# Order of the attention heads in the second half of a two-branch decoder layer, with its side products spread anew and one scaling moved to ScalarE

## The chip, the cores and the metric

One core of a Trainium2 chip runs the whole layer in one launch. The metric is the device time of that execution in microseconds. PE is TensorE (matmuls), PEld its weight loads, DVE VectorE, ACT ScalarE, POOL GpSimd, SP SyncE, which here issues the DMAs.

## The reference

The input x is 2048 tokens of 1024 channels in fp32. After an RMS norm, one projection gives queries, keys, values and gates of two attention branches and two more gates of 1024 columns each:

```python
h = rms_norm(x, pre_norm_g)
(sb_q, sb_k, sb_v, sb_z, df_q, df_k, df_v, df_z, g_sb, g_df) = split_cols(h @ w_in)
# stick-breaking branch, 8 heads of 64, block of queries against all keys before them
z = q @ k.T * scale
a = exp(log_sigmoid(z) - suffix)        # suffix: sum of softplus(z) over the later keys
y_sb = ((a @ v) * silu(sb_z)) @ w_o_sb
# differential branch, 4 heads, two score maps each, ALiBi bias, causal
p = softmax(s + bias)
y_df = (rms_norm((p[0] - lam * p[1]) @ v, subln_g) * 0.8 * silu(df_z)) @ w_o_diff
merged = sigmoid(g_sb + b) * y_sb + sigmoid(g_df + b) * y_df
out = x + rms_norm(merged @ w_out, post_norm_g)
```

## The kernel before, in words

Products are made in a split form: an operand is kept as a rounded part and a rest, and a product is the sum of three (or two) matmuls. A projection of 128 columns for 512 tokens is 24 matmuls (8 chunks of channels by 3), and one call of a generator makes one of them; a pair of calls covers the 1024 tokens of a half and shares one loaded weight tile (`load_w`, tags `w_hi` and `w_lo`, two buffers each).

The sequence is worked in two halves of 1024 tokens. In each, the list `heads` (line 1056) names the attention heads in order: a stick-breaking entry is a pair of heads (names s00 to s13, the first digit being the half), a differential one is a head with two maps (d00 to d13). While one is in attention, the projections of the next are interleaved (q, k, v and, for stick-breaking, z), in the order of the letters of `ORDER`. The letter S in it stands for the side steps: the differential gates' projections (z, 8 calls a half) and those of the two merge gates (g, 32 calls a half). `SIDES` says how many of the 40 fall to each of the eight entries of a half. In the second half the last 16 steps (`LAST_G`) are ordered by token group: eight for the first 512 tokens, then eight for the others, each with its own weight load.

Stick-breaking attention (`sb_group`): scores into PSUM, a sigmoid on ScalarE, a running product on VectorE (`a_R`, a scan), split into two f16 parts (`a_W`), a transposing DMA (`a_P`), a scaling copy to fp32r (`a_h`; three of four by ScalarE, the fourth by GpSimd), the product with the values (`a_O`). Differential attention (`df_row`): scores, bias and maximum on VectorE, exponentials on ScalarE (`f_row`), then row 1 scaled by `l2` and added to row 0. Chunks of even number do that in one VectorE instruction, chunks of odd number in two on GpSimd. `df_pair` transposes the sum on TensorE (`f_T`), splits it (`f_h`, `f_l`) and multiplies (`f_O`).

Behind the last head stands the merge of 256 tokens at a time (`merge`: products `y` with w_o, gates by a sigmoid; `finish`: products `o` with w_out and the norm). Its first four groups of tokens need only the first half's results. The matrix w_o is loaded in two halves into the buffers of the normed input (`load_wo`): the first when the last head starts, the second when the last side step is recorded. w_out (`load_wout`) goes to the buffers of the attention. In the last head the side steps are spread over the first 70% of its work.

The program is recorded first (`Recorder`), then put in order (`plan`): a list scheduler that knows a cost for every instruction (`cost`), and, for each buffer tag, how many of the next tiles in line may be taken (`FREE`: three for the PSUM tag "pj" of projections and of `y`, one otherwise). `issue` writes the instructions out in that order, and each engine runs its own in order.

Of the kernel before, what the change touches and what calls it, by code (L numbers as in the profile page):

```python
# [13 lines left out]
AF = mybir.ActivationFunctionType  # L14
ALU = mybir.AluOpType
# [19 lines left out]
FBANKS = ("S", "T", "S", "T", "S", "O", "pj")  # L35
HBANKS = (("S", "T"), ("S", "T"))
XTAGS = (("V",) * 4, ("row", "row", "row", "pre"))
SIDES = ((4, 4, 4, 4, 4, 4, 4, 12), (4, 4, 4, 4, 4, 4, 4, 12))
LAST_G = (2, 8)
SCALE = 0.125  # L40
LAMBDA_INIT = 0.2
SLOPES = [2.0 ** (-8.0 * (h + 1) / NDIFF) for h in range(NDIFF)]
BIG = 1e30
RSCALE = 2.0 ** 15
OFF = dict(sb_q=0, sb_k=512, sb_v=1024, sb_z=1536, df_q=2048, df_k=2560, df_v=3072, df_z=3584, g=4096)


# [84 lines left out]
class Recorder:  # L132


    def __init__(self, nc):
        self.nc, self.ops, self.lane, self.fifo, self.hold = nc, [], 0, {}, None
        for e in ENGINES:
            setattr(self, e, _Engine(self, e))

    def tile(self, pool, shape, dtype, name, tag=None, bufs=None, depth=None):  # L140
        t = Tile_(pool, tag, bufs, shape, dtype, name)
        if depth:
            t.free = self.fifo.setdefault((id(pool), tag), [depth, [], depth])
        return View(t)
# [65 lines left out]
def cost(o):  # L210

    v = o.outs[0] if o.outs else o.ins[0]
    n = 1
    for k in (o.ins[0] if o.call in ("tensor_reduce",) else v).shape[1:]:
        n *= k
    if o.engine == "tensor":
        t = 109.0 if o.call == "transpose" else 5 + 0.4415 * max(n, 256)
        return t, n / 2.4 + 215
    psum = any(x.tile.tag in ("S", "T", "O", "pj") for x in o.ins)
    if o.engine == "scalar":  # L220
        t = 80 + 0.833 * n + (80 if any(isinstance(o.kw.get(k), View) for k in ("scale", "bias")) else 0)
        if "accum_out" in o.kw:
            return t + 130, t + 260
        return t, t + 100
    if o.engine == "vector":
        if n <= 8:
            return 195.0, 200.0
        if o.call == "tensor_tensor_scan":
            t = 60 + 2.36 * n
        elif o.call in ("tensor_scalar", "tensor_scalar_mul", "tensor_scalar_add", "tensor_copy", "memset") and not psum:  # L230
            t = 130 + 0.7 * n
        elif o.call == "tensor_tensor_reduce":
            return 75 + 1.06 * n, 230 + 1.06 * n
        else:
            t = (75 if psum else 135) + 1.07 * n
        return t, t + 75
    if o.engine == "gpsimd":
        if any(isinstance(a, View) for a in o.args[2:]) and o.call == "tensor_scalar":
            return 280 + 2.5 * n, 330 + 2.5 * n
        t = {"tensor_tensor": 100 + 2.3 * n, "tensor_sub": 100 + 2.3 * n, "tensor_add": 100 + 2.3 * n, "memset": 180 + 0.2 * n}.get(o.call, 190 + 0.9 * n)  # L240
        return t, t + 50
    if o.kw.get("transpose"):
        return 1250.0, 3400.0
    size = 4.0 * 128 * n
    return 70.0, 2100 + size / 150

FREE = {"pj": 3}
# [6 lines left out]
def plan(rec):  # L256

    import heapq

    now, order = 0.0, []  # L260
    free = dict.fromkeys(ENGINES, 0.0)
    waiting = {e: [] for e in ENGINES}
    ripe = {e: [] for e in ENGINES}
    events, n_event = [], 0
    dma = 0.0
    live = {}
    blocked = {}
    port = {"vector": 0.0, "gpsimd": 0.0}

    def can_take(o):  # L270
        for t in o.new:
            q = t.free
            if q is None or t.real == "held":
                continue
            if q[0] <= 0 or t not in q[1][:FREE.get(t.tag, 1)]:
                return q
        return None

    def offer(o):
        heapq.heappush(waiting[o.engine], (o.ready + o.spare, o.n, o))  # L280
        heapq.heappush(events, o.ready)
        heapq.heappush(events, o.ready + o.spare)

    for o in rec.ops:
        if not o.left:
            offer(o)
    done = 0
    while done < len(rec.ops):
        progress = False
        for e in ENGINES:  # L290
            if free[e] > now:
                continue
            w, r = waiting[e], ripe[e]
            while w and w[0][0] <= now:
                _, _, o = heapq.heappop(w)
                heapq.heappush(r, (o.prio, o.n, o))
            put_back, took = [], None
            while r:
                x = heapq.heappop(r)
                q = can_take(x[2])  # L300
                if q is None:
                    took = x[2]
                    break
                blocked.setdefault(id(q), (q, []))[1].append(x)
            if took is None:
                early = min((x for x in w if x[2].ready <= now and can_take(x[2]) is None), default=None)
                if early is None:
                    continue
                w.remove(early)
                heapq.heapify(w)  # L310
                took = early[2]
            o = took
            progress = True
            o.start = max(now, port["gpsimd" if e == "vector" else "vector"]) if o.port else now
            free[e] = o.start + o.took * MARGIN[e]
            if o.port:
                port[e] = free[e]
            if e == "sync":
                dma = max(dma, now) + (o.lag - 2100) * 0.6
                o.end = dma + 2100  # L320
            else:
                o.end = o.start + o.lag * MARGIN[e]
            order.append(o)
            done += 1
            for t in o.new:
                if t.free is not None:
                    t.free[1].remove(t)
                    t.free[0] -= 1
                    wake(blocked, t.free, ripe, heapq)
            for s in (*o.succ.values(), *o.behind.values()):  # L330
                spare = 0.0
                if s.n in o.behind:
                    at = now
                elif s.engine == e and e != "sync":
                    at = free[e]
                else:
                    at, spare = o.end + HOP, SAFE[s.engine]
                    if s.engine == "tensor" and s.call == "transpose":
                        at += STATIONARY
                s.spare = max(s.ready + s.spare, at + spare)  # L340
                s.ready = max(s.ready, at)
                s.spare -= s.ready
                s.left -= 1
                if not s.left:
                    offer(s)
            for t in {v.tile for v in (*o.outs, *o.ins)}:
                t.users -= 1
                live[t] = max(live.get(t, 0.0), o.end)
                if not t.users and t.free is not None:
                    n_event += 1  # L350
                    heapq.heappush(events, live[t] + HOP)
                    heapq.heappush(blocked.setdefault("ends", []), (live[t] + HOP, n_event, t.free))
            heapq.heappush(events, free[e])
        if progress:
            continue
        assert events, stuck(blocked)
        now = max(now, heapq.heappop(events))
        ends = blocked.get("ends", [])
        while ends and ends[0][0] <= now:
            q = heapq.heappop(ends)[2]  # L360
            q[0] += 1
            wake(blocked, q, ripe, heapq)
    return order
# [27 lines left out]
def hybrid_layer(ctx: ExitStack, tc: tile.TileContext, x, pre_g, w_in, b_gate, lq1, lk1, lq2, lk2, subln_g, w_o_sb, w_o_df, w_out, post_g, out):  # L391
# [329 lines left out]
    def sb_group(p, hf, hd, gl, K, V, q, u):  # L721
# [4 lines left out]
        for kc in range(G, -1, -1):  # L726
            edge = kc == G
            ends = sm([P, 4], F32, name=f"{n}_e{kc}", tag="ends")
            for half in range(2):
# [25 lines left out]
                for j in range(nj):  # L755
# [2 lines left out]
                    hl = T([P, 2, CQ], F32R, f"{n}_h{kc}{half}{j}", tag)  # L758
                    if c0:
                        nc.gpsimd.memset(hl[:, :, :c0].bitcast(F32), 0.0)  # L760
                    if j == 3:
                        nc.gpsimd.tensor_scalar(hl[:, :, c0:], post[:, j, :, c0:], 1.0 / RSCALE, 0.0, ALU.mult, ALU.add)
                    else:
                        nc.scalar.activation(hl[:, :, c0:], post[:, j, :, c0:], AF.Copy, scale=1.0 / RSCALE)
                    lhs = V[kc // 2][:, (kc % 2) * 4 + j, :]
# [11 lines left out]
    def sb_attend(p, hf, st):  # L777
        us = [T([P, CH], F32, f"u{hf}{p}{gl}", "u") for gl in range(2)]
        zs = zb_dram[p][:, hf * HALF:(hf + 1) * HALF]
        early = (hf, p) not in ((0, 3), (1, 1))  # L780
        if early:
            zt = T([P, 2, CH], F32, f"uz{hf}{p}", "bm")
            nc.sync.dma_start(zt, zs)
# [41 lines left out]
    def df_row(d, hf, ii, st, bias, l1):  # L825
# [37 lines left out]
        for k, (c, w) in enumerate(ck):  # L863
# [1 line left out]
            if k % 2 == 0:  # L865
                nc.vector.scalar_tensor_tensor(a, b, l2, a, ALU.mult, ALU.add)
            else:
                nc.gpsimd.tensor_scalar(b, b, l2, None, ALU.mult)
                nc.gpsimd.tensor_add(a, a, b)
        return {(c + o) // P: rows[0][k][:, o:o + P] for k, (c, w) in enumerate(ck) for o in range(0, w, P)}  # L870

# [176 lines left out]
    with tc.tile_pool(name="wpool", bufs=2, reuse_waits="tile") as wpool, tc.tile_pool(name="att", bufs=1, reuse_waits="tile") as apool:  # L1048
# [4 lines left out]
        build_h(0, 0, xs[0])  # L1053
        load_constants()
        xs.append(load_x(0, 1, XTAGS[1]))
        heads = [(hf, sb, i) for hf, sb, pairs in ((0, 1, range(4)), (0, 0, range(4)), (1, 1, range(2)), (1, 0, range(4)), (1, 1, range(2, 4))) for i in pairs]
        project = lambda hf, sb, i: (sb_project if sb else df_project)(i, hf)

        def do(f):
# [14 lines left out]
        for k, (hf, sb, i) in enumerate(heads):  # L1074
# [46 lines left out]
                sides = side(1)  # L1121
            st = st2
        assert not sides
        M = merge(0, wo)
        rec.hold = None
        wt = load_wout()
# [37 lines left out]
```

## Time and profile before

| | |
|---|---|
| median of 3 runs | 2184.78 us (2184.68 to 2186.52) |
| the profiled execution | 2185.57 us |
| its span, first to last instruction | 2183.8 us |
| TensorE busy in the span | 2077.5 us, 95% |
| VectorE, ScalarE, GpSimd busy | 62%, 56%, 40% |
| mean granted TensorE clock | 0.982 |

The span is what the trace shows; the time holds 1.8 us more around it. Matmuls are pipelined and a record's end is modelled, so a busy TensorE is not yet one at its peak; the number of instructions in a stretch says more.

### The profile page before, as it was taken

The numbers are of one execution on the slowest core, as the hardware profiler recorded it, in microseconds if no ns is written. First come the engines' busy times: TensorE is split into PE (matmuls) and PEld (weight loads), VectorE is DVE, ScalarE is ACT, GpSimd is POOL, SyncE is SP. The second block draws the span as 40 slices with busy tenths as digits, with TensorE's granted clock in tenths as the row PEclk, the third lists the DMA queues.
The fourth block names the chain that finished last, engine by engine and source line by source line (L and its number), as shares of the span: only waits on it lengthen the run. The fifth ranks groups of instructions, "written<-read, shape, count | busy, mean of one in ns | idle before, by whom it ended". The sixth has DMA issues, their size and how long they took to land.

```text
span 2183.8 us, 34416 instructions
## 1 busy us (share of the span) xinstructions
PE 2077.5 (95%) x11136; PEld 1766.1 (81%) x11136; DVE 1356.7 (62%) x3142; ACT 1220.9 (56%) x2937; POOL 876.9 (40%) x1086
## 2 busy tenths in 40 slices
PE   5999999999999999999989999999998978999998
PEld 5888888888888888777878888888876767988997
DVE  6546655656557467777776767776775575434344
ACT  4556565644444478888655555656886674322221
POOL 2556566655354124444434243433444564111110
PEclk9999999999999999999999999999999989999999
DMA  5987988854564479979523232325899987444542
GB/s 157 273 235 207 272 210 247 225 189 163 190 237 162 135 190 206 200 167 203 150 63 118 70 112 78 104 72 151 194 231 247 285 165 184 141 144 134 161 131 87
DMA packets 474083, 376.26 MB, mean 172 GB/s; under 512 B 309552, under 2 KB 391472, under 8 KB 473904
## 3 DMA queue, kind: packets, MB, share of 16 engines
q1 hardware_dynamic: 473904, 374.07, 62.7%
q8 instruction: 88, 1.44, 0.3%
q14 instruction: 91, 0.75, 0.1%
HBM read 168.44 MB, written 117.44 MB: 131 GB/s over the span
## 4 chain that ended last, share of the span: by engine, by line
PE 42%; ACT 6%; DMA 5%; DVE 3%; issue 2%; POOL 1%; SPq 1%; DVEq 0%; ACTq 0%; POOLq 0%
PE y L384 7%; PE o L384 7%; PE g L384 6%; DMA a_P<-a_W 4%; PE f_S L384 3%; PE f_O L384 3%; PE a_O L384 2%; PE a_S L384 2%; PE f_T L384 2%; ACT f_row L384 1%; ACT a_h L384 1%; SPq L384 1%; ACT a_W L384 1%; DMA u<-ul_dram 1%; DVE f_row L384 1%
## 5 line engine op out<-in xcount | busy, mean ns | idle before, releaser
L384 POOL TENSOR_TENSOR a_W<-a_R,a_W 128x512 f16<-128x512 f32 (+1 forms) x160 | 182.7, 1143 | 225.4 <-ACT a_W L384 205.9
L384 ACT ACTIVATE a_h<-a_P 128x512 fp32r<-128x512 f16 (+1 forms) x448 | 244.0, 606 | 33.8 <-DMA a_P<-a_W 20.4
L384 DVE TENSOR_TENSOR_SCAN a_R<-a_S,a_e,high 128x512 f32<-128x512 f32 x192 | 237.7, 1269 | 35.5 <-ACT a_S L384 20.6
L384 ACT ACTIVATE f_row<-f_row,f_mx 128x512 f32<-128x512 f32 (+3 forms) x320 | 206.9, 652 | 51.0 <-DVE f_mx L384 50.8
L384 PE MATMUL y<-u,woh 128*128 128x256 f32 x1024 | 209.8, 284 | 3.4 <-DVE y04g L384 2.3
L384 PE MATMUL g<-hh,g_w_hi 128*128 128x512 f32 x512 | 203.5, 397 | 3.7 <-ACT g_s L384 2.2
L384 PE MATMUL g<-hh,g_w_lo 128*128 128x512 f32 x512 | 203.9, 398 | 1.3 <-DMA g_w_lo<-g_w_d 1.2
L384 PE MATMUL o<-wt,m 128*128 128x512 f32 x672 | 203.9, 396 | 0.0
L384 PE MATMUL g<-hl,g_w_hi 128*128 128x512 f32 x512 | 203.4, 397 | 0.0
L384 ACT ACTIVATE a_W<-a_R 128x512 f16<-128x512 f32 (+2 forms) x320 | 174.2, 556 | 28.3 <-DMA a_P<-a_W 22.1
L384 DVE CUSTOM_DVE_ANT_0 f_row<-f_S,f_bm 128x512 f32<-128x512 f32 (+3 forms) x304 | 167.1, 573 | 34.1 <-PE f_T L384 16.6
L384 PEld LDWEIGHTS y<-u,woh 128*128 128x128 f32 x1024 | 169.7, 191 | 11.3 <-issue 3.0
L384 DVE TENSOR_TENSOR a_W<-a_R,a_W 128x512 f16<-128x512 f32 (+2 forms) x160 | 115.8, 725 | 100.6 <-ACT a_W L384 98.7
L384 POOL TENSOR_SCALAR f_row<-f_row,f_l 128x512 f32<-128x512 f32 (+2 forms) x64 | 109.5, 1711 | 153.3 <-DVE f_l L384 149.1
L384 ACT ACTIVATE f_h<-f_T 128x512 fp32r<-128x512 f32 (+2 forms) x176 | 81.9, 497 | 128.1 <-PE f_T L384 55.0
L384 PE MATMUL y<-u,wol 128*128 128x256 f32 x512 | 142.5, 283 | 0.0
L384 PEld LDWEIGHTS o<-wt,m 128*128 128x128 f32 x672 | 123.1, 190 | 23.4
L384 DVE TENSOR_TENSOR f_l<-f_T,f_h 128x512 fp32r<-128x512 f32 (+2 forms) x176 | 94.8, 565 | 68.5 <-ACT f_h L384 66.6
L384 DVE TENSOR_TENSOR_SCAN a_R<-a_R,high 128x128 f32<-128x128 f32 (+3 forms) x128 | 112.8, 910 | 35.7 <-POOL a_R L384 34.9
L384 ACT ACTIVATE a_S<-a_S 128x512 f32<-128x512 f32 x192 | 107.9, 578 | 34.2 <-PE a_S L384 32.9
L384 POOL TENSOR_SCALAR a_h<-a_P 128x512 fp32r<-128x512 f16 (+1 forms) x128 | 83.4, 652 | 82.8 <-PE a_O L384 37.9
L384 PEld LDWEIGHTS g<-hh,g_w_hi 128*128 128x128 f32 x512 | 97.1, 190 | 21.6 <-ACT g_s L384 3.5
(1182 smaller groups left out, 5622.2 us busy)
## 6 DMA issues: line engine op xcount, KB each, us to landing
g_dram<-g_s SPq DMA_DIRECT2D x64, 256.0 KB, 3.1
g_w_hi<-g_w_d SPq DMA_DIRECT2D x24, 512.0 KB, 3.7
g_w_lo<-g_w_d SPq DMA_DIRECT2D x24, 512.0 KB, 5.0
g_w_raw<-in_w_in_dram SPq DMA_DIRECT2D x32, 256.0 KB, 4.0
g_w_d<-g_w_hi SPq DMA_DIRECT2D x16, 512.0 KB, 4.1
g_w_d<-g_w_lo SPq DMA_DIRECT2D x16, 512.0 KB, 4.4
u<-uh_dram SPq DMA_DIRECT2D x64, 128.0 KB, 3.2
u<-ul_dram SPq DMA_DIRECT2D x64, 128.0 KB, 3.4
```

The costliest lines, as they stand in the source:

```text
L384: i = getattr(getattr(rec.nc, o.engine), o.call)(*map(real, o.args), **{k: real(v) for k, v in o.kw.items()}).ins
```

## The change

In the second half the four stick-breaking entries come first and the four differential ones behind them; before, two stick-breaking ones stood on either side of the differential ones. The side steps of that half are 5, 5, 5, 5, 4, 4, 4, 8 instead of seven times 4 and 12. The stick-breaking entry that stands ahead of a differential one is now s13, so s13 loads its gate late (`early`) and s11 early. The odd chunks of row 1 are scaled by ScalarE; the addition stays on GpSimd. In the planner, a DMA issue costs 420 ns instead of 70, a transposing one 1320 instead of 1250, and tiles carry a stage: a tile of the merge can't be taken while an earlier stage's tile of the same tag is still in line. `SHARE` writes the old choice of engine for the copy of the fourth block as a table and changes nothing.

```diff
-SIDES = ((4, 4, 4, 4, 4, 4, 4, 12), (4, 4, 4, 4, 4, 4, 4, 12))
+SIDES = ((4, 4, 4, 4, 4, 4, 4, 12), (5, 5, 5, 5, 4, 4, 4, 8))
+SHARE = ((0, 0, 0, 1), (0, 0, 0, 1))
...
-        self.nc, self.ops, self.lane, self.fifo, self.hold = nc, [], 0, {}, None
+        self.nc, self.ops, self.lane, self.fifo, self.hold, self.stage = nc, [], 0, {}, None, 0
...
         t = Tile_(pool, tag, bufs, shape, dtype, name)
+        t.stage = self.stage
...
     if o.kw.get("transpose"):
-        return 1250.0, 3400.0
+        return 1320.0, 3400.0
     size = 4.0 * 128 * n
-    return 70.0, 2100 + size / 150
+    return 420.0, 2100 + size / 150
...
-            if q[0] <= 0 or t not in q[1][:FREE.get(t.tag, 1)]:
+            if q[0] <= 0 or t not in q[1][:FREE.get(t.tag, 1)] or q[1][0].stage != t.stage:
                 return q
...
-                    if j == 3:
-                        nc.gpsimd.tensor_scalar(hl[:, :, c0:], post[:, j, :, c0:], 1.0 / RSCALE, 0.0, ALU.mult, ALU.add)
+                    if SHARE[half][j]:
+                        (None, nc.gpsimd, nc.vector)[SHARE[half][j]].tensor_scalar(hl[:, :, c0:], post[:, j, :, c0:], 1.0 / RSCALE, 0.0, ALU.mult, ALU.add)
...
-        early = (hf, p) not in ((0, 3), (1, 1))
+        early = (hf, p) not in ((0, 3), (1, 3))
...
-                nc.gpsimd.tensor_scalar(b, b, l2, None, ALU.mult)
+                nc.scalar.activation(b, b, AF.Copy, scale=l2)
                 nc.gpsimd.tensor_add(a, a, b)
...
-        heads = [(hf, sb, i) for hf, sb, pairs in ((0, 1, range(4)), (0, 0, range(4)), (1, 1, range(2)), (1, 0, range(4)), (1, 1, range(2, 4))) for i in pairs]
+        heads = [(hf, sb, i) for hf, sb, pairs in ((0, 1, range(4)), (0, 0, range(4)), (1, 1, range(4)), (1, 0, range(4))) for i in pairs]
...
         assert not sides
+        rec.stage = 1
         M = merge(0, wo)
```

## Rows read from the trace of the kernel before

**Rows 1.** The page: TensorE's share, then granted clock and DMA in 40 slices.

```profile
PE 2077.5 (95%) x11136; PEld 1766.1 (81%) x11136; DVE 1356.7 (62%) x3142; ACT 1220.9 (56%) x2937; POOL 876.9 (40%) x1086
...
PEclk9999999999999999999999999999999989999999
DMA  5987988854564479979523232325899987444542
```

**Rows 2.** Busy time by head: s10, s11, d10 to d13, s12, s13 in two parts.

```profile
core 0: us, PE busy (x) PEld busy (x) DVE busy (x) ACT busy (x) POOL busy (x), PEclk, DMA share, GB/s
765.40:907.00 141.60, 140.68 (x714) 118.12 (x713) 96.05 (x126) 112.03 (x257) 51.47 (x71) 1.00 0.85 198
907.00:1039.50 132.50, 119.84 (x582) 97.62 (x581) 97.63 (x113) 111.54 (x257) 58.88 (x78) 0.94 0.86 186
1039.50:1139.90 100.40, 94.22 (x511) 79.58 (x511) 74.39 (x230) 60.50 (x154) 37.38 (x40) 0.98 0.40 110
1139.90:1264.10 124.20, 120.26 (x674) 102.45 (x673) 90.62 (x282) 68.85 (x187) 49.15 (x48) 0.99 0.28 90
1264.10:1379.40 115.30, 111.66 (x633) 95.46 (x632) 84.72 (x268) 65.79 (x178) 44.24 (x45) 1.00 0.30 97
1379.40:1511.00 131.60, 128.02 (x708) 109.36 (x707) 93.77 (x288) 79.84 (x206) 51.01 (x49) 0.99 0.34 104
1511.00:1644.30 133.30, 127.90 (x657) 106.83 (x658) 100.61 (x135) 111.19 (x262) 51.43 (x75) 0.97 0.88 207
1644.30:1760.00 115.70, 106.44 (x534) 86.53 (x533) 66.10 (x76) 79.06 (x178) 57.31 (x72) 1.00 1.03 256
```

**Rows 3.** The same: merge, last slice, d03, all of s13, and the first half.

```profile
1856.20:2129.20 273.00, 272.38 (x1760) 246.99 (x1759) 113.72 (x307) 68.09 (x152) 39.01 (x51) 1.00 0.46 142
2129.20:2183.80 54.60, 46.11 (x242) 39.25 (x240) 23.17 (x76) 9.02 (x23) 2.96 (x4) 0.95 0.27 87
...
652.80:728.00 75.20, 73.28 (x374) 61.48 (x373) 41.59 (x163) 28.39 (x82) 28.48 (x31) 0.98 0.47 162
1644.30:1850.00 205.70, 172.50 (x894) 142.80 (x893) 128.03 (x151) 129.99 (x288) 108.30 (x133) 0.94 0.93 223
57.00:764.60 707.60, 702.44 (x3572) 592.32 (x3571) 415.77 (x1079) 376.31 (x924) 368.52 (x476) 1.00 0.72 211
```

**Rows 4.** Waits from 1640 to 1860 us: total us, times, longest us.

```profile
PE a_O L384 <- ACT a_h L384: 19.7, 11, 4.3
ACT a_W L384 <- DMA a_P<-a_W: 14.9, 14, 2.0
...
ACT y07g L384 <- DMA y07g<-g_dram: 5.1, 1, 5.1
```

**Rows 5.** Timeline of SyncE: start, us, what is issued, how many.

```profile
1645.30 1.31 SPq L384 DMA_TRANSPOSE a_P<-a_W  x1
...
1648.03 2.00 SPq L384 DMA_DIRECT2D u<-uh_dram  x4
```

**Rows 6.** The chain that ended last: start, us, one side step.

```profile
1741.19 5.48 PE g L384 x24
```

**Rows 7.** Groups of instructions, whole span: busy us, mean ns, idle before.

```profile
L384 POOL TENSOR_SCALAR f_row<-f_row,f_l 128x512 f32<-128x512 f32 (+2 forms) x64 | 109.5, 1711 | 153.3 <-DVE f_l L384 149.1 <-ACT g_s L384 4.1
...
L384 ACT ACTIVATE hh<-hps,gpre 128x512 fp32r<-128x512 f32 x32 | 19.5, 698 | 7.2 <-PE hps L384 7.1
...
L384 ACT ACT_TABLE_LOAD x10 | 12.8, 1283 | 2.8 <-DVE f_mx L384 1.9 <-PEq L1150 0.7
```

**Rows 8.** TensorE's waits from 1039 to 1512 us.

```profile
PE f_T L384 <- DVE f_row L384: 4.5, 2, 3.3
```

**Rows 9.** DMA issues of a weight tile: count, size, us to landing.

```profile
g_w_hi<-g_w_d SPq DMA_DIRECT2D x24, 512.0 KB, 3.7
g_w_lo<-g_w_d SPq DMA_DIRECT2D x24, 512.0 KB, 5.0
```

## The prediction, made before the changed kernel was run

> **What bounds the kernel now.** I read the page first. TensorE is busy 95% of the span, nothing else is near [rows 1]. But a share over the span hides stages, so I cut the second half at each head's first score product and asked for each stretch. The reader is to see two things in [rows 2]. First, the three stretches of differential heads from 1039.5 to 1379.4 us (d10, d11, d12) and the one of stick-breaking head s10 are nearly full of matmuls: TensorE idle 0.9 us in s10, about 4 to 6 us in each of the others. Second, s11 and s12 take 132.5 and 133.3 us although s12 holds 75 more TensorE instructions (657 against 582). So a stick-breaking head of this half lasts about 133 us whatever the TensorE work is, up to some 655 instructions: it is paced by its own chain (score, sigmoid, scan, split, DMA transpose, copy, product) on ScalarE, which is busy for 111 to 112 us in each of the three whole heads, with the DMA engines at 0.85 to 0.88. In s11 TensorE is idle 12.7 us and its granted clock is 0.94, that is, part of the stretch ran at 1.2 GHz after such gaps.
>
> The last stick-breaking head, s13, is the worst place. From 1644.3 to 1850.0 us TensorE is idle 33.2 us of 205.7 at clock 0.94 [rows 3]. The waits there are the stick-breaking chain's: products wait 19.7 us for ScalarE's copies, which wait for transposes [rows 4]. DMA share is 1.03 in the first part of it, since w_o and w_out are loaded under the transposes [rows 2]. After 1856 us the merge runs without loss: 1760 instructions in 273.0 us, 0.155 us each, at clock 1.00 [rows 3].
>
> **The change, part by part.** I add stretches of the new order in the profiled execution's own span, 2183.8 us, and at the end the 1.8 us that the execution (2185.57) has around it; the median of the runs shown, 2184.78, is 0.8 us below that execution.
>
> Everything up to 765.4 us keeps its work. The planner's new costs for SyncE (70 to 420 ns for a copy, 1250 to 1320 for a transpose) reorder the program there too; the trace has 0.50 us a copy and 1.31 us a transpose [rows 5], so the plan comes nearer to the chip. Whether that gains or loses no row shows. From 57.0 to 764.6 us TensorE idles only 5.2 us in all at clock 1.00 [rows 3], so the gain is bounded by 5; a loss of the same size is the other end. I take nothing.
>
> s10: one more side step. A step is 24 matmuls, 5.5 us in the chain [rows 6]. TensorE is full here, so 141.6 + 5.5 = 147.1.
>
> s11: it now projects s12 instead of d10: the gate projection is new, 48 matmuls, and there are five steps instead of four, 24. 582 + 72 = 654, nearly what s12 held in 133.3 us. I take 133. If nothing were absorbed it would be 132.5 + 72 x 0.228 (5.48 us / 24) = 148.9; that is the other end.
>
> s12: by the code its own work is 320 attention matmuls, 8 transposes, 8 x 24 of projection and 4 x 24 of side steps, 616; the other 41 of its 657 were the end of d13, which goes. One more step: 640, and s11's remainder. 133, upper end 138.8.
>
> s13: now followed by d10, so it projects without a gate: 320 + 8 + 6 x 24 + 5 x 24 = 592, like s11's 582 before. 133. Before, the same head with twelve steps and the weights of both output matrices took 539.5 us together with the merge (1644.3 to the end). Of that the merge's own 2304 matmuls (8 x 8 x 24 and 8 x 2 x 2 x 24) at 0.155 are 357.4, and the last slice loses 54.6 - 242 x 0.155 = 17.1 [rows 3]. So s13 took 165.0: 32 us go from this stretch.
>
> d10, d11, d12: four steps each as before: 100.4 + 124.2 + 115.3 = 339.9. The second map's odd chunks are scaled by ScalarE instead of GpSimd: 64 instructions of 1711 ns (109.5 us in all) leave GpSimd [rows 7]. What they cost ScalarE no row shows; the nearest is the copy with a per-partition scale, 698 ns from PSUM, and by it 12 a head are 8.4 us. In d11 ScalarE is busy 68.9 of 124.2, so that is covered by its idle time; without that cover it would be 8 us a head. The row's chain gets 1 us shorter, but TensorE waits only 4.5 us in all for these rows [rows 8], so I take nothing (bounds: 4.5 us won, 8 us a head lost).
>
> d13: before, 708 instructions, of them 8 x 24 + 8 for projecting s12 and 4 x 24 of side steps. Now no projection and eight steps: 708 - 200 - 96 + 192 = 604, and its own end, 41, which before lay in s12: 645. At d12's 115.3 us / 633 = 0.182 us this is 117.5, against 131.6.
>
> End of d13: all steps are placed in the first 70% of the head; behind them the only filler is the merge, which the new stage mark lets take a PSUM bank only after the last step has one. w_o's first half can load at once, since just the steps of the second token group are left; DMA share in these heads is 0.28 to 0.40, so it does not meet transposes. The output weights still wait for the head's V and row buffers. The row for this hand-over in the differential form is the first half's last one, 652.8 to 728: 1.9 us idle and 0.02 x 75 of clock, 3.4 [rows 3]; the row in the stick-breaking form is the old tail, 32. I take 12, nearer to the former because there is no transpose in the chain, and keep 5 and 32.
>
> A held buffer: five steps break a pair that shares its weights. The pair's tile stays in one of two buffers from s10 into s11, and from s12 into s13, so the projections between load one behind the other. A load lands 3.7 and 5.0 us after its issue [rows 9]. About two loads a time are uncovered by other steps; attention covers a third: 2 x 2 x 5 x 2/3 = 13 at most. s12 to s13 has slack, so I take 4.
>
> Sum: 765.4 + 147.1 + 3 x 133 + 339.9 + 117.5 + 357.4 + 17.1 + 12 + 4 = 2159.4, with 1.8 around it 2161.2. The merge can fill about 1 us of d13's own gaps; 2160.
>
> **A rule that speaks against it.** Ten table loads of 1283 ns each are in the whole execution [rows 7]: heads of one kind follow each other and the function set seldom changes. The new last head does exponentials while the merge's gates want a sigmoid. The Trainium skill, "ScalarE: Activation LUTs", section "Table sets: the hidden batching unit", says to group activations by set; the trace's 1283 ns is the page's own figure for the load, and with the drain that the page adds (about 2.66 us together) sixteen switches would be about 43 us of queue time, an estimate from that page, by which the sum would come to some 2178 where the rows' 20.5 us (16 x 1.283) lets it stand at 2160. The trace shows no drain as an instruction. By rows alone the same mechanism, with the waits behind it, is the slower rival below.
>
> **Rivals.** (1) Everything is absorbed: the hand-over costs 5, the hold nothing, the merge fills 7 us of d13's idle time and the DMA transposes wait less: 2160 - 7 - 4 - 6 = 2143, down to 2135. For it: DMA idle in differential heads. Against: the merge's own evictions queue behind exponentials. (2) The stick-breaking heads absorb nothing: 15.9 + 5.8 more, 2182. For it: DMA share at 0.85 already, and one more step and a gate load more. Against: s12's 657 in 133.3. This is also the case in which the change does nothing. (3) Slower: the last head stalls in ScalarE's in-order queue. Each of the eight first gates stands between exponentials, takes two table loads (2.57 us) and may wait at the head of the queue for its load, 5.1 us in the worst case before [rows 4]: 8 x (2.57 + 5.1) = 61 us. In the last 40% of the head (47 us) ScalarE's own work is about 0.61 x 47 (79.84 of 131.6 in d13 [rows 2]) and 5 for the merge's share, 34, so 48 us do not fit; 12 of them are in the forecast as the hand-over: 2160 + 36 = 2196. It decides once about 38 us of queue time do not fit. Against it: the plan may put gates behind the last exponential, where they cost nothing.
>
> **How the numbers follow.** Forecast (2150 to 2174) 0.55; rival 1 0.15; rival 2 (2175 to 2189) 0.17; rival 3 0.13. 0.2%, 4.4 us, is about what a measurement of this kernel tells from no change. Faster: 0.55 + 0.15 + 0.09 of rival 2 = 0.79; same 0.07; slower 0.14. The range takes in rival 1's end and most of rival 2 and 3: 2135 to 2189; the forecast's own is 2150 to 2174.
>
> **What would show it.** Four stretches of about 147, 133, 133, 133 us with TensorE idle under 8 us in the middle two; DMA share under 1.0 there; GpSimd's row scaling gone and a ScalarE one of about 0.6 to 0.7 us; d13 near 118 us; less than 15 us lost at its end; ScalarE table loads between 10 and 20. It is wrong if a stick-breaking stretch exceeds 140, if the clock falls in s11 as before, or if table loads pass 20 and products wait for exponentials at the end.

## The result, and the profile after

The changed kernel takes 2150.78 us (median of 4 runs, 2150.61 to 2151.29); the kernel before, on the same chip, 2185.65. The ratio is 0.984, interval 0.9823 to 0.9857. The forecast was 2160; the change gained 34.9 us where 25.6 (2185.57 to 2160) were forecast.

Busy time of the changed kernel in the stretches from one head's first score product to the next one's: s10, s11, s12, s13, d10, d11, d12, then d13 up to the first output product, the hand-over, the merge and the last slice.

```profile
core 0: us, PE busy (x) PEld busy (x) DVE busy (x) ACT busy (x) POOL busy (x), PEclk, DMA share, GB/s
768.70:917.90 149.20, 146.88 (x743) 122.91 (x742) 103.94 (x133) 116.23 (x266) 53.95 (x74) 1.00 0.83 193
917.90:1052.60 134.70, 126.01 (x638) 102.87 (x637) 98.69 (x122) 113.30 (x260) 58.32 (x77) 1.00 0.91 197
1052.60:1188.60 136.00, 126.93 (x638) 105.13 (x637) 97.13 (x118) 113.61 (x262) 58.40 (x77) 0.97 0.92 191
1188.60:1321.50 132.90, 121.05 (x590) 99.66 (x589) 92.06 (x107) 110.29 (x253) 55.64 (x76) 0.95 0.88 193
1321.50:1425.30 103.80, 102.86 (x571) 88.18 (x570) 76.34 (x245) 72.51 (x178) 29.52 (x40) 1.00 0.41 113
1425.30:1538.80 113.50, 111.83 (x636) 96.25 (x635) 83.95 (x266) 74.29 (x193) 27.83 (x37) 1.00 0.35 117
1538.80:1660.10 121.30, 116.93 (x661) 100.87 (x660) 91.14 (x276) 79.53 (x205) 32.40 (x38) 0.99 0.39 128
1660.10:1771.20 111.10, 105.85 (x625) 91.78 (x623) 84.14 (x262) 70.76 (x184) 34.24 (x42) 1.00 0.54 172
1771.20:1821.20 50.00, 48.47 (x321) 43.53 (x322) 35.64 (x63) 17.26 (x39) 24.79 (x30) 0.97 0.48 148
1821.20:2094.20 273.00, 271.69 (x1752) 245.78 (x1751) 117.87 (x305) 68.14 (x150) 39.51 (x51) 1.00 0.46 141
2094.20:2148.80 54.60, 46.15 (x246) 39.45 (x245) 24.55 (x77) 9.35 (x24) 4.07 (x5) 0.95 0.26 87
```

The rows answer to [rows 2, 3]. The reader is to see three things. The stick-breaking stretches last 149, 135, 136 and 133 us with 638, 638 and 590 instructions in the last three: s11, which had 582 in 132.5 us, took in 56 more for 2.2 us. The stretches d10 to d12 take 338.6 us with 1868 instructions, where before they took 339.9 with 1818: they too carry more in the same time. (These are sums of three rows; an instruction that crosses an edge is counted in both, so one row over all three has 4 less.) And the hand-over to the merge, idle for 33.2 of 205.7 us before, now idles 5.3 of 111.1 and 1.5 of 50.0.

Term by term, in the span. The merge here is 2304 x 273.0 / 1752 = 359.0 and the last slice's loss 54.6 - 246 x 0.156 = 16.3.

| stretch | forecast | measured |
|---|---|---|
| up to s10 | 765.4 | 768.7 |
| s10, s11, s12, s13 | 147.1 + 3 x 133 = 546.1 | 552.8 |
| held buffer | 4 | within the row above |
| d10, d11, d12 | 339.9 | 338.6 |
| d13 and hand-over | 117.5 + 12 = 129.5 | 488.7 - 375.3 = 113.4 |
| merge and last slice | 374.5 | 375.3 |

### The profile page after: what moved, and what is told of

Read it like the earlier page. It is cut to its first block, busy times and chain, and to the rows that moved or that the text cites. A ratio compares the mean times of both kernels' runs of the same rounds, so it can differ in the third digit from the quotient of the medians.

```text
span 2148.8 us, 34389 instructions
## 1 busy us (share of the span) xinstructions
PE 2064.1 (96%) x11136; PEld 1758.2 (82%) x11136; DVE 1365.7 (64%) x3142; ACT 1258.7 (59%) x2999; POOL 779.7 (36%) x1022
## 4 chain that ended last, share of the span: by engine, by line
PE 37%; ACT 4%; DMA 4%; DVE 3%; issue 2%; POOL 1%; SPq 1%; DVEq 0%; ACTq 0%; POOLq 0%
PE y L386 7%; PE o L386 7%; PE g L386 5%; PE f_S L386 4%; PE f_O L386 3%; PE a_O L386 2%; PE f_T L386 2%; DMA a_P<-a_W 2%; PE a_S L386 1%; ACT a_h L386 1%; ACT f_row L386 1%; ACT a_W L386 1%; DVE f_row L386 1%; SPq L386 1%; DMA u<-ul_dram 1%
## 5 line engine op out<-in xcount | busy, mean ns | idle before, releaser
L386 ACT ACTIVATE a_h<-a_P 128x512 fp32r<-128x512 f16 x448 | 243.9, 608 | 22.9 <-DMA a_P<-a_W 20.3
L386 PE MATMUL o<-wt,m 128*128 128x512 f32 x672 | 199.3, 395 | 3.1 <-ACT m L386 2.4
L386 POOL TENSOR_TENSOR f_row<-f_row,f_row 128x512 f32<-128x512 f32 (+2 forms) x64 | 78.2, 1232 | 159.1 <-ACT f_row L386 158.3
## 6 DMA issues: line engine op xcount, KB each, us to landing
u<-uh_dram SPq DMA_DIRECT2D x64, 128.0 KB, 3.2
u<-ul_dram SPq DMA_DIRECT2D x64, 128.0 KB, 3.6
```

Source lines behind the costliest of these rows:

```text
L386: i = getattr(getattr(rec.nc, o.engine), o.call)(*map(real, o.args), **{k: real(v) for k, v in o.kw.items()}).ins
```

## The experiments

Times are medians; each ratio is to the kernel before, run on the same chip. The runs are from several chips, on which the kernel before took 2185.3 to 2187.4 us, so a difference of 2 us between runs of different groups says nothing.

**Order alone.** All of the change but the planner's SyncE costs and the scaling on ScalarE.

```diff
-        return 1320.0, 3400.0
+        return 1250.0, 3400.0
...
-    return 420.0, 2100 + size / 150
+    return 70.0, 2100 + size / 150
...
-                nc.scalar.activation(b, b, AF.Copy, scale=l2)
+                nc.gpsimd.tensor_scalar(b, b, l2, None, ALU.mult)
```

> The changed kernel with the planner's SyncE costs (70 and 1250 ns) and the GpSimd scaling of before: order of heads, side steps and stage mark alone. Order theory (the gain comes from the new order): within 5 us of the changed kernel's 2150.8, since both other parts were taken at nothing. Planner theory (the new DMA costs give it): no better than 2175. GpSimd theory (freeing GpSimd of 109 us gives it): no better than 2170.

2145.18 us, ratio 0.9819 (0.9802 to 0.9835): 40 us of gain, 5.6 better than the whole change. So the order, with its side steps and the stage mark, is what gains. It also seems to beat the whole, though the two intervals overlap; if it does, one of the other two parts costs.

**Planner's SyncE costs, with the stage mark.** The kernel before with 420 and 1320 ns. With the new costs alone the planner finds no order at all (products of the merge and side steps block each other's PSUM banks), so the stage mark goes with them, and this run does not tell the two apart.

```diff
-        return 1250.0, 3400.0
+        return 1320.0, 3400.0
...
-    return 70.0, 2100 + size / 150
+    return 420.0, 2100 + size / 150
...
-            if q[0] <= 0 or t not in q[1][:FREE.get(t.tag, 1)]:
+            if q[0] <= 0 or t not in q[1][:FREE.get(t.tag, 1)] or q[1][0].stage != t.stage:
...
+        rec.stage = 1
```

> The kernel before with the new SyncE costs in the planner and the stage mark, nothing else. Order theory: 2185.7 within 5 us. Planner theory: 2160 or less. In the profile of the changed kernel the second half starts 3.3 us later than before (768.7 against 765.4), which by the order theory is this part's doing: then the same 3 us show here ahead of the first score product of s10.

2196.43 us, ratio 1.0043 (1.0028 to 1.0059): slower by about 10. The second half starts at 771.8 us, 6.4 later than before. The part that I took at nothing costs.

**Scaling on ScalarE alone**, in the kernel before.

```diff
-                nc.gpsimd.tensor_scalar(b, b, l2, None, ALU.mult)
+                nc.scalar.activation(b, b, AF.Copy, scale=l2)
```

> The kernel before with the odd chunks' scaling on ScalarE, nothing else. Order theory: 2185.7 within 4 us, since TensorE waited 4.5 us in all for the rows and ScalarE has idle time in the differential heads. GpSimd theory: 2170 or less. If the cover on ScalarE is missing: up to 8 us for each of the four heads of the second half, 2217.

2171.92 us, ratio 0.9938 (0.9924 to 0.9952): 13.4 us of gain where the order theory had at most 4 and the GpSimd theory 15 or more. The order theory is out; the GpSimd theory's 2170 lies just inside the interval. The stretch of d10 to d12, whose work on TensorE is the same in both kernels, before and then with this one edit:

```profile
1039.50:1379.40 339.90, 326.13 (x1814) 277.49 (x1814) 249.73 (x777) 195.14 (x518) 130.78 (x132) 0.99 0.32 98
```

```profile
1039.40:1363.50 324.10, 320.98 (x1814) 275.90 (x1813) 243.03 (x778) 218.43 (x558) 81.50 (x108) 1.00 0.33 103
```

The stretch gets 15.8 us shorter: TensorE's idle time falls from 13.8 to 3.1 us, and the granted clock rises from 0.99 to 1.00. ScalarE's waits for the transposed rows in that stretch, then TensorE's waits for copies by ScalarE, before:

```profile
ACT f_h L384 <- PE f_T L384: 27.6, 15, 3.4
...
PE d12q_ps L384 <- ACT d12vt L384: 1.8, 1, 1.8
PE d11q_ps L384 <- ACT d11vt L384: 1.8, 2, 1.2
PE d13q_ps L384 <- ACT d13vt L384: 1.8, 1, 1.8
```

And with the edit:

```profile
ACT f_h L384 <- PE f_T L384: 4.8, 6, 1.7
```

ScalarE waited 27.6 us at the head of its queue for the transposes of finished rows, and now waits 4.8. TensorE waited 13.7 us in all in the stretch, 9.2 of them for copies by ScalarE such as d12vt, under names that have nothing to do with the row; with the edit it waits 2.9. But it was not those waits of ScalarE that the copies stood behind. Ahead of d12vt, before, ScalarE waited for VectorE's `f_u` and then did the eight exponentials of a row without a gap:

```profile
1232.86 0.63 ACT L384 ACTIVATE f11us_uh<-f_u 128x512 fp32r<-128x512 f32 x1 [4.86 <-DVE f_u L384]
...
1238.12 0.49 ACT L384 ACTIVATE f_row<-f_row,f_mx 128x256 f32<-128x256 f32 x1
...
1239.09 0.58 ACT L384 ACTIVATE d12vt<-d12v_ps 128x512 f32<-128x512 f32 x1
```

The same stands ahead of d13vt, and exponentials or the squares of the norm ahead of most others. So ScalarE's queue held TensorE up; that late rows had filled that queue is not shown. What the edit does to a row can be read off: from the factor `l2` to the row's last addition it took 3.8 us in this half's rows with one odd chunk and 5.8 in those with two, and takes 2.6 and 3.6 with the edit. The edit costs ScalarE 654 ns each, 40.3 us in all, and that does not lengthen the stretch:

```profile
L384 ACT ACTIVATE f_row<-f_row,f_l 128x512 f32<-128x512 f32 (+2 forms) x64 | 40.3, 654 | 25.5 <-DVE f_l L384 25.1
```

**Ending with a differential head, but in turns**: s10 s11 d10 d11 s12 s13 d12 d13. The side steps go by place in the list, so d10 and d11 get five here and s12 and s13 four. Two stick-breaking heads now stand ahead of a differential one, so both load their gate late.

```diff
-        early = (hf, p) not in ((0, 3), (1, 3))
+        early = (hf, p) not in ((0, 3), (1, 1), (1, 3))
...
-(1, 1, range(4)), (1, 0, range(4)))
+(1, 1, range(2)), (1, 0, range(2)), (1, 1, range(2, 4)), (1, 0, range(2, 4)))
```

> The changed kernel with the second half's order s10 s11 d10 d11 s12 s13 d12 d13: it ends with a differential head but does not put four stick-breaking heads in a row. If the last head's kind is what counts, it keeps the hand-over's gain (28 of about 35 us in my stretches) and lands at 2150 to 2160. If four stick-breaking heads in a row are needed so that each takes in the next one's longer projections, s11 falls back to 582 matmuls with idle time and the time is 2165 or more.

2178.05 us, ratio 0.996 (0.9945 to 0.9975). The kind of the last head alone is not enough. It does bring most of the gain at the end: from d13 to the end this run takes 498.7 us, the changed kernel 488.7. Nor is it quite the second theory: s11 fell back to 592 instructions, but in 123.3 us. Most of the loss lies in d10 and d11, which carry five steps each and, in d11, the longer projections of s12. s11, d10 and d11:

```profile
917.60:1040.90 123.30, 116.87 (x592) 95.85 (x591) 93.47 (x106) 108.12 (x250) 55.00 (x75) 1.00 0.91 204
...
1040.90:1163.10 122.20, 114.20 (x607) 94.83 (x606) 86.38 (x257) 78.60 (x193) 35.85 (x45) 0.96 0.36 97
1163.10:1308.90 145.80, 138.82 (x763) 118.42 (x762) 92.33 (x289) 83.05 (x212) 20.92 (x24) 0.98 0.31 105
```

1370 instructions in 268.0 us are 0.196 us each; in the changed kernel's d10 to d12 it is 338.6 / 1868 = 0.181. At 0.181 they would take 248, so this makes 20 us of the 27 between the two kernels. ScalarE loads tables 14 times here and 8 times in the changed kernel. Which of the three (steps, projections, tables) weighs most was not separated.

**Old planner costs** in the changed kernel.

```diff
-        return 1320.0, 3400.0
+        return 1250.0, 3400.0
...
-    return 420.0, 2100 + size / 150
+    return 70.0, 2100 + size / 150
```

> The changed kernel with the planner's SyncE costs put back to 70 and 1250 ns; order, side steps, stage mark and ScalarE scaling stay. If the parts add up as they did alone (order 2145.2, scaling 13.5 us won in the old order, planner costs 10 us lost), it lands at 2132 to 2140. If the scaling's gain was tied to the old order, whose differential heads stood between stick-breaking ones, it stays at 2143 to 2151.

2134.17 us, ratio 0.9765 (0.975 to 0.9779). The parts add up: order 40, scaling 11 more, and the planner's costs take 16.6 back. This version beats both kernels. The stretch s11 to s13 of the changed kernel, then of this one:

```profile
917.90:1321.50 403.60, 373.99 (x1860) 307.66 (x1859) 287.87 (x346) 337.20 (x773) 172.36 (x229) 0.97 0.90 194
```

```profile
917.80:1306.80 389.00, 367.89 (x1852) 303.81 (x1851) 288.95 (x345) 333.30 (x768) 168.27 (x227) 0.98 0.91 199
```

14.6 us lie there, with the same work. Behind it the new costs lose 7.1 us more in d10 to d12 and gain 6.4 from d13 to the end, as some work moves from there into d10 to d12.

**No pair of steps split.** Same number of steps in the four stick-breaking heads.

```diff
-(5, 5, 5, 5, 4, 4, 4, 8))
+(4, 6, 4, 6, 4, 4, 4, 8))
```

> The changed kernel with side steps 4, 6, 4, 6, 4, 4, 4, 8 instead of 5, 5, 5, 5, 4, 4, 4, 8: the same twenty steps in the four stick-breaking heads, but no pair of steps is split over two heads, so no weight buffer is held. Held-buffer theory: 4 us faster, at most 13. If the hold costs nothing: within 3 us of 2150.8, or slower where s11, which gets six, is less able to take them than s10.

2147.9 us, ratio 0.9822 (0.9805 to 0.9839), 2.9 faster than the changed kernel, whose interval it overlaps; that lies between the two theories. The four stretches sum to 552.6 us against 552.8 there: s10, which lost a step, is 9 us shorter, and s11, which got one, 10 longer:

```profile
908.10:1053.10 145.00, 132.96 (x664) 110.28 (x663) 105.78 (x126) 117.68 (x270) 63.91 (x81) 0.96 0.87 187
```

So the sum of the heads in which the buffer is held shows no cost of it; what the step costs s11 and what the hold would are not told apart.

**The old side steps** in the new order.

```diff
-(5, 5, 5, 5, 4, 4, 4, 8))
+(4, 4, 4, 4, 4, 4, 4, 12))
```

> The changed kernel with the side steps of before, 4 in each head and 12 in the last. Absorption theory: four steps leave the stick-breaking heads, where about 17 of their 22 us were hidden, for the last differential head, which is full of matmuls: about 2165, d13 some 22 us longer and s11 to s13 no shorter. If the stick-breaking heads did not absorb them, nothing changes: 2151 within 4.

2169.03 us, ratio 0.9924 (0.9905 to 0.9943): 18.3 us lost. s11, with 612 instructions, still lasts 141 us, and d13 grows to 139.6 us at clock 1.00. The third row is s11 to s13 together:

```profile
909.60:1050.70 141.10, 124.76 (x612) 102.75 (x611) 101.55 (x125) 113.11 (x262) 58.76 (x78) 0.95 0.84 182
1660.80:1800.40 139.60, 138.03 (x814) 120.31 (x813) 96.70 (x278) 76.47 (x194) 46.21 (x55) 1.00 0.59 186
...
909.60:1325.90 416.30, 378.29 (x1860) 311.72 (x1858) 296.47 (x353) 342.09 (x784) 177.88 (x236) 0.94 0.86 186
```

About half of the gain (18.3 of 34.9 us) is thus the spread of the steps. One thing does not fit the absorption theory: s11 to s13 hold as many instructions as in the changed kernel, 1860, as work of the heads behind moves up into them (d10 holds 462 there and 571 in the changed kernel), yet last 416.3 us where they lasted 403.6, at clock 0.94 instead of 0.97. Why was not found.

**GpSimd's scaling without the planner's exclusion**, on the run with the order alone.

```diff
+        if o.engine == "gpsimd" and call == "tensor_scalar" and any(isinstance(a, View) for a in args[2:]):
+            o.port = False
```

> The run with the order alone (2145.2; GpSimd scales the odd chunks), in which only the planner no longer lets that GpSimd instruction and VectorE exclude each other; the instructions are the same, their order is planned anew. If the gain of moving the scaling came from the plan, which holds VectorE back for 1.7 us at each of the 64, it gains as much as the move does in this order. If it came from the chip (a row that is ready 1 us sooner, a shorter GpSimd queue), the time stays at 2145 within 3 us or rises, as the plan is now too hopeful.

2144.3 us, ratio 0.982 (0.9802 to 0.9838), against 2145.2. Lifting the exclusion gains nothing, so the scaling's gain does not come from it. As the order is planned anew in every run, this rules out the exclusion and not every effect of the plan.

**Scaled on ScalarE, and once more on GpSimd behind the addition**, on the version of 2134.2.

```diff
                 nc.gpsimd.tensor_add(a, a, b)
+                nc.gpsimd.tensor_scalar(b, b, l2, None, ALU.mult)
```

> The kernel with old planner costs and ScalarE scaling (2134.2), to which each of the 64 odd chunks adds the GpSimd scaling of before once more, behind the addition and into a row that nobody reads any longer: GpSimd is as busy as it was, but the row is ready as early as with ScalarE. The extra product changes no result. Chain theory (the row being ready 1 us earlier is what gained 11 us): 2134 to 2138. Occupancy theory (GpSimd's queue and VectorE slowed beside it): back to 2143 to 2147.

2135.65 us, ratio 0.9759 (0.9743 to 0.9776). GpSimd's load is back, 89.8 us of the 109.5 in [rows 7], and costs nothing:

```profile
L386 POOL TENSOR_SCALAR f_row<-f_row,f_l 128x512 f32<-128x512 f32 (+2 forms) x64 | 89.8, 1403 | 6.4
```

So the length of GpSimd's queue is not what cost. But the expectation was wrong about the row: where a row has two odd chunks, the extra scaling of the first stands ahead of the addition of the second:

```profile
1390.03 1.70 POOL L386 TENSOR_TENSOR f_row<-f_row,f_row 128x512 f32<-128x512 f32 x1 [3.26 <-ACT f_row L386]
1391.83 1.57 POOL L386 TENSOR_SCALAR f_row<-f_row,f_l 128x512 f32<-128x512 f32 x1
1393.36 0.74 POOL L386 TENSOR_TENSOR f_row<-f_row,f_row 128x256 f32<-128x256 f32 x1
```

From `l2` to the last addition such rows, half of those of the second half, take 5.3 us here, 3.8 in the base and 5.9 in the run with the order alone; those with one odd chunk take 2.6 here and 2.5 in the base. So half the rows were nearly as late as with GpSimd's scaling, and the time stayed: that the row being ready earlier is what gains is not shown by this run. Nor did VectorE's slowing come back (733 ns on average, last section), so that rival is untested. What in the move gains stays open.

**No stage mark**, on the same version.

```diff
-            if q[0] <= 0 or t not in q[1][:FREE.get(t.tag, 1)] or q[1][0].stage != t.stage:
+            if q[0] <= 0 or t not in q[1][:FREE.get(t.tag, 1)]:
```

> The same base (2134.2) without the stage mark, so that products of the merge may take PSUM banks while side steps are still in line. If the mark matters for the hand-over, the merge's first products hold banks while they wait for their gates and 5 us or more are lost. In the base the first product of the merge comes 18 us ahead of the first output product; if the mark does little, 2134 within 3.

2133.68 us, ratio 0.9756 (0.9735 to 0.9778): the mark is worth nothing here.

**More steps in the stick-breaking heads**, on the same version, in two sizes.

```diff
-(5, 5, 5, 5, 4, 4, 4, 8))
+(4, 6, 6, 8, 4, 4, 4, 4))
```

> The same base with side steps 4, 6, 6, 8, 4, 4, 4, 4: four more steps in the stick-breaking heads, and more of them in s12 and s13, which still have TensorE idle 6.5 and 8.9 us. Absorption theory: four steps (22 us) leave d13 and one leaves s10, about half of that is hidden, 2120 to 2128. If s11 to s13 are full by now: 2134 within 4, or slower where the split of work starves the last head of filler.

```diff
-(5, 5, 5, 5, 4, 4, 4, 8))
+(2, 8, 8, 8, 4, 4, 4, 2))
```

> The same base with 2, 8, 8, 8, 4, 4, 4, 2: twenty-six steps in the stick-breaking heads. They hold 640 + 72 matmuls then, near 710, 0.2 us each is 142 us: past what a 130 us head can hide. Expected no better than the run before, 2125 to 2140; a stick-breaking head longer than 140 us would show the limit of what it absorbs.

2141.73 us (0.979, 0.9774 to 0.9806) and 2141.97 us (0.9794, 0.9775 to 0.9814): 7.6 and 7.8 slower than their base, which ran on another chip; by the ratios it is 5.5 and 6.3. I was wrong about the first. The first one's s11, s13 and d13, then the second one's s11 and d13:

```profile
906.80:1046.00 139.20, 131.64 (x663) 110.48 (x662) 107.08 (x127) 116.73 (x267) 60.13 (x80) 0.96 0.87 195
...
1181.10:1321.30 140.20, 134.22 (x690) 112.86 (x691) 95.67 (x110) 121.46 (x273) 62.79 (x85) 0.99 0.94 199
1658.50:1763.50 105.00, 94.04 (x569) 80.06 (x567) 86.41 (x254) 64.68 (x165) 37.28 (x46) 0.95 0.44 138
```

```profile
907.80:1055.70 147.90, 140.78 (x708) 116.31 (x707) 105.66 (x132) 121.42 (x276) 63.41 (x82) 0.98 0.88 194
1670.50:1777.50 107.00, 94.67 (x601) 84.75 (x599) 86.51 (x261) 78.31 (x182) 38.87 (x48) 0.94 0.37 115
```

Stick-breaking heads with 663 to 708 instructions take 135 to 148 us, and d13 starves: it idles 11 to 12 us of 105 to 107, and its clock falls to 0.94 to 0.95. In the first of the two, the four steps add 14.7 us to the stick-breaking heads (553.9 against 539.2 in the base), their leaving takes 15.0 from d13 to the end, and d10 to d12 get 5.7 longer: the move gains nothing. What keeps d13 at 105 us with 569 instructions was not tested.

## Why the prediction was right, and where it was not

The direction, the place and the main terms held. A stick-breaking stretch of about 133 us that takes in filler up to some 655 instructions is what the traces of the changed kernel show, three times within 3 us of the forecast. As a rule it is looser than I wrote: with 592 to 664 instructions such a stretch took from 123.3 us (s11 of the order in turns) to 145.0 (s11 without split pairs).

The fairest test of the sum is the run with the order alone, since the other two edits stood in it at nothing. Its s10 to s13, d10 to d12, and d13 to the end, then the same of the version with old planner costs, which adds the scaling:

```profile
765.60:1307.80 542.20, 516.84 (x2597) 429.65 (x2596) 393.77 (x476) 450.37 (x1033) 221.37 (x301) 0.98 0.89 196
1307.80:1639.70 331.90, 325.71 (x1824) 277.05 (x1823) 248.01 (x771) 200.25 (x525) 134.32 (x137) 1.00 0.38 118
1639.70:2144.60 504.90, 482.07 (x2986) 427.75 (x2984) 262.38 (x725) 168.22 (x405) 137.18 (x154) 0.99 0.46 142
```

```profile
767.60:1306.80 539.20, 515.49 (x2597) 428.77 (x2596) 391.52 (x476) 449.87 (x1033) 224.65 (x301) 0.98 0.89 197
1306.80:1638.30 331.50, 327.16 (x1843) 280.42 (x1842) 245.70 (x781) 222.69 (x566) 85.79 (x109) 1.00 0.39 120
1638.30:2133.40 495.10, 474.64 (x2967) 423.93 (x2965) 261.66 (x714) 170.38 (x410) 107.12 (x134) 0.99 0.46 144
```

| stretch | forecast | order alone |
|---|---|---|
| up to s10 | 765.4 | 765.6 |
| s10 to s13, held buffer | 546.1 + 4 = 550.1 | 542.2 |
| d10 to d12 | 339.9 | 331.9 |
| d13 to the end | 129.5 + 374.5 = 504.0 | 504.9 |

So d13 with its hand-over was sized right for the order. The 16 us by which it is shorter in the changed kernel come with the two edits that I took at nothing: with the scaling this stretch loses 9.8 us, while 19 of its instructions move up into d10 to d12, which take no longer for it; with the new planner costs it loses another 6.4 (495.1 to 488.7), as 28 more move up. Mis-sized by 8 us each were the stick-breaking heads with the held buffer, and d10 to d12: I took these at their old length, and in the new order TensorE idles 6.2 us in them where it idled 13.8. What the order changed there was not found.

Two edits that I took at nothing were not nothing. The scaling is worth 11 us in the new order and 13.4 in the old, outside the bound of 4.5, because I bounded it by the waits that TensorE has by name for the row. I also took the row's chain as 1 us shorter, where it gets 1.2 to 2.2 us shorter. TensorE felt ScalarE's queue, under the names of other copies; how much of the gain is the earlier row, VectorE no longer slowed beside GpSimd's scaling, or another plan, the runs do not separate. The planner's SyncE costs lose 16.6 us, outside the bound of 5, and most of it in the stick-breaking heads, not in the first half that I bounded it by. Numbers nearer to the chip's gave a worse plan. Why was not found: in s11 to s13 both versions' tables of waits have much the same entries on top, and the waits of GpSimd's copies for TensorE's products are the most clearly longer with the new costs (43.7 us against 24.4). That stays open. Without them s11, s12 and s13 last 130.8, 130.2 and 128.0 us, so my 133 was right for a slower plan than I had in mind.

That the total came within 10 us is in part luck: the order gained 15 us more than forecast and the scaling 11, and the planner's costs took 16.6 back.

The held buffer was put at 4 us. The run without it is 2.9 us faster, not clear of noise, and the heads in which it is held sum to the same; whether it costs anything is not settled.

Some of the signs that I named missed without harm: TensorE idles 8.7 and 9.1 us in s11 and s12 where I asked for under 8, d13 takes 111.1 us where I wrote about 118, and there are 8 table loads where I wrote 10 to 20. The clock stays at 1.00 in s11 but falls to 0.95 in s13. One sign was badly chosen: a stick-breaking stretch over 140 us was to show the forecast wrong, while s10 was itself forecast at 147 (149.2 measured). And rival 3's 2196 lies above the 2189 at which the range ends.

The slower rival did not come about. ScalarE's activations around the first gate of the merge in the changed kernel:

```profile
1761.81 1.28 ACT L386 ACT_TABLE_LOAD   x1 [1.35 <-DMA y00g<-g_dram]
1763.10 0.63 ACT L386 ACTIVATE y00g<-y00g 128x512 f32<-128x512 f32 x1
1763.75 1.28 ACT L386 ACT_TABLE_LOAD   x1
1765.05 0.73 ACT L386 ACTIVATE f_row<-f_row,f_mx 128x512 f32<-128x512 f32 x1
```

One gate stands among the exponentials, and the plan put the others behind the last of them: 8 loads in the whole execution, fewer than the 10 before. The rule of the Trainium skill, "ScalarE: Activation LUTs", section "Table sets: the hidden batching unit", to group activations by set, is thus kept by the plan without knowing it. The same page of the Trainium skill adds a drain of about 1.38 us to a load, in its section "What ACT_TABLE_LOAD costs". Here the second load starts 0.02 us after the gate's sigmoid ends, and the exponential 1.30 us after that load starts, so the trace shows no such drain and a switch costs the 1.28 us of the load.

## What to carry to other kernels

Price a move by what the stretches at its two ends can take in: a head paced by its own chain swallows filler until its matmuls fill its length, which here still differed by some 10 us from plan to plan, and a head that runs out of filler can lose the clock as well. Before an edit of an off-path engine is put at nothing, try it alone: the waits by name on the busiest engine understate it (4.5 us here for 13), as they name the copy that came last in a queue and not what filled the queue. Measure the parts of a compound change alone, the planner's constants too: one of three here cost 16.6 us, and without it the kernel takes 2134.2 instead of 2150.8.

## What the runs showed of the hardware that was not expected

The same GpSimd scaling of a full chunk took 1991 ns on average in the kernel before, where it ran beside VectorE's scaling of the neighbouring chunk, and 1622 ns in the run with both scalings, where it came later (a span on GpSimd is rough):

```profile
L384 POOL TENSOR_SCALAR f_row<-f_row,f_l 128x512 f32<-128x512 f32 x40 | 79.6, 1991 | 127.8 <-DVE f_l L384 127.6
```

```profile
L386 POOL TENSOR_SCALAR f_row<-f_row,f_l 128x512 f32<-128x512 f32 x40 | 64.9, 1622 | 3.9
```

VectorE's own instruction, scaling and adding the even chunks, took 898 ns on average for a full chunk in the kernel before and 786 ns with the scaling moved and nothing else changed:

```profile
L384 DVE SCALAR_TENSOR_TENSOR f_row<-f_row,f_l,f_row 128x512 f32<-128x512 f32 x64 | 56.1, 898 | 1.7
```

```profile
L384 DVE SCALAR_TENSOR_TENSOR f_row<-f_row,f_l,f_row 128x512 f32<-128x512 f32 x64 | 49.0, 786 | 1.7
```

The Trainium skill, "GPSIMD Engine Reference", section "8. Key points", says that GpSimd shares its SBUF interfaces with VectorE and contends with VectorE instructions that have two SBUF inputs. The rows agree in direction; over all widths VectorE's 96 instructions take 77.5 us before and 68.6 in the run with this edit alone. It is no even slowing. In the kernel before, 55 full chunks were scaled by VectorE beside GpSimd's scaling and nothing else: the 39 that VectorE began first took 750 to 754 ns, as long as with GpSimd idle (750), and the 16 that it began while GpSimd's was running took 1176 to 1183. The run with the order alone has the same two groups, 36 of 750 to 753 ns and 16 of 1175 to 1184. What the contention costs the kernel was not tried by itself: in the run with both scalings GpSimd's stands behind the addition, and VectorE's mean over all widths there is 733 ns.
